# A small early write of zeros to the output, and the last store moved to the SP queue, in a one-core lp-pool kernel

## The chip, the cores and the metric

The kernel runs on one core of a Trainium2 chip. The metric is the time of the kernel on the device in microseconds (us), the median of several executions. A profiled execution also leaves a trace, whose span (first to last instruction) is some 2 us shorter than the time; where this text says "span" it means the trace.

## The reference, cut to what matters

An lp pooling with p = 2 over windows of 4: square, mean over 4 neighbours, square root. The input is 32 x 256 x 4096 float32 (134.22 MB), the output a quarter of it (33.55 MB).

```python
for i in range(out_length):
    window = np.abs(x[:, :, 4 * i:4 * i + 4]) ** 2.0
    result[:, :, i] = np.mean(window, axis=-1) ** 0.5
```

## The kernel before

The input is taken as 32 loads of 4 MB (128 partitions x 8192 floats, 32 KB a row), all issued by the sync engine SP into four slots. Each load is squared in place by ScalarE (ACT), in two halves, summed in fours by VectorE (DVE) into an output tile, and rooted by ACT. Four loads fill one output tile of 4 MB. The first six such tiles are stored from ACT's DMA queue; the last two big ones (called held) are stored from SP's queue, after all loads have been issued; the last output block comes from a single load, is 1 MB, and is stored from ACT.

```python
in_pool = ctx.enter_context(tc.tile_pool(name="in_pool", bufs=4))
out_pool = ctx.enter_context(tc.tile_pool(name="out_pool", bufs=2))
last_pool = ctx.enter_context(tc.tile_pool(name="last_pool", bufs=1))
# [cut]
def root(i, c):
    # [cut]
    nc.scalar.activation(
        out=o, in_=o, func=mybir.ActivationFunctionType.Sqrt, scale=1.0 / k,
    )
    if i == first + g - 1 and c + CH == W and group_of[i] not in held:
        nc.scalar.dma_start(out=out_block(group_of[i]), in_=ot)

for i in range(3):
    load(i)

pending = None
for i in range(n):
    if i + 3 < n:
        load(i + 3)
    # [cut] square, sum, and the root of the half before
root(*pending)
for gi in sorted(held):
    nc.sync.dma_start(out=out_block(gi), in_=ots[gi])
```

## Time and profile before

| before | value |
|---|---|
| time, median | 395.79 us (3 runs, 395.79 to 395.8) |
| span of the trace | 393.7 us |
| bytes moved by DMA | 167.79 MB, mean 426 GB/s over the span |
| DVE / ACT busy | 72% / 75% |

First lines of the page. The digits are the busy tenths of the 16 DMA engines in 40 equal slices (9.84 us each), and GB/s is what they moved in each slice.

```profile
span 393.7 us, 357 instructions
...
DVE 282.8 (72%) x64; ACT 294.7 (75%) x130; POOL 0.2 (0%) x4
...
DMA  8999998999999999999999999999999999999997
GB/s 350 446 430 426 426 426 373 449 446 430 433 426 426 426 430 453 440 430 433 426 426 426 426 449 443 427 433 430 426 426 426 443 446 433 430 433 426 426 435 314
DMA packets 5906, 167.79 MB, mean 426 GB/s; under 512 B 656, under 2 KB 656, under 8 KB 656
```

The reader is to see that the DMA engines are busy from end to end, and that one slice stands out: the seventh, 59 to 69 us, at 373 GB/s where its neighbours have 426 or more.

The longest waits of the two compute engines (engine, line and tile, what was waited for: total us, times, longest).

```profile
DVE ot L112 <- ACT xt L108: 102.6, 38, 16.5
ACT xt L108 <- DMA xt<-in_x_dram: 85.0, 32, 10.9
```

ACT waits for loads, DVE for ACT: the compute engines follow the DMA.

Some lines of the chain of work that ended last, in order of time (start us, us, what).

```profile
2.11 39.87 DMA xt<-in_x_dram
...
54.55 37.06 DMA xt<-in_x_dram
...
104.18 35.91 DMA xt<-in_x_dram
...
152.67 35.95 DMA xt<-in_x_dram
...
249.70 36.50 DMA xt<-in_x_dram
...
347.26 26.27 DMA xt<-in_x_dram
```

A "DMA" entry here is the stretch until a load landed. Nearly the same pattern repeats every 48.5 us, with a load stretch of 35.9 us. Two are longer: the second, which spans the first store (37.06 us), and the sixth (36.50 us). The first, with the start in it, and the last, for one load alone, can't be compared.

The DMA issues of the page (out<-in, queue, count, size of each, median us from issue to landing).

```profile
xt<-in_x_dram SPq DMA_DIRECT2D x32, 4096.0 KB, 35.9
out_dram<-ot ACTq DMA_DIRECT2D x6, 4096.0 KB, 23.2
out_dram<-ot SPq DMA_DIRECT2D x1, 4096.0 KB, 34.1
out_dram<-ot SPq DMA_DIRECT2D x1, 3072.0 KB, 12.3
out_dram<-ot ACTq DMA_DIRECT2D x1, 1024.0 KB, 5.6
```

Below the page lie the records of the single DMA packets. An undisturbed 32 KB load packet takes 1.213 us on one engine. This text calls the *loss* of a stretch the sum of what packets there took above the undisturbed time of their size (1.213 us for 32 KB, 0.912 for 24 KB, 0.309 for 8 KB; only packets over 2% above it count), divided by the 16 engines. Around the first store of this kernel, between 30 and 66 us, that is 1.14 us, of which 1.12 lie between 58 and 62 us. From 66 to 345 us, with five more big stores from ACT's queue, it is 0.06 us.

### The profile page before, as it was taken

The numbers are of one execution on the slowest core, as the hardware profiler recorded it, in microseconds if no ns is written. First come the engines' busy times: TensorE is split into PE (matmuls) and PEld (weight loads), VectorE is DVE, ScalarE is ACT, GpSimd is POOL, SyncE is SP. The second block draws the span as 40 slices with busy tenths as digits, with TensorE's granted clock in tenths as the row PEclk, the third lists the DMA queues.
The fourth block names the chain that finished last, engine by engine and source line by source line (L and its number), as shares of the span: only waits on it lengthen the run. The fifth ranks groups of instructions, "written<-read, shape, count | busy, mean of one in ns | idle before, by whom it ended". The sixth has DMA issues, their size and how long they took to land.

```text
span 393.7 us, 357 instructions
## 1 busy us (share of the span) xinstructions
DVE 282.8 (72%) x64; ACT 294.7 (75%) x130; POOL 0.2 (0%) x4
## 2 busy tenths in 40 slices
DVE  0399996739976399764988559866598846999992
ACT  1699987469883798828988189863998819999981
POOL 0000000000000000000000000000000000000000
DMA  8999998999999999999999999999999999999997
GB/s 350 446 430 426 426 426 373 449 446 430 433 426 426 426 430 453 440 430 433 426 426 426 426 449 443 427 433 430 426 426 426 443 446 433 430 433 426 426 435 314
DMA packets 5906, 167.79 MB, mean 426 GB/s; under 512 B 656, under 2 KB 656, under 8 KB 656
## 3 DMA queue, kind: packets, MB, share of 16 engines
q1 hardware_dynamic: 4896, 141.56, 83.9%
q10 hardware_dynamic: 1008, 26.21, 15.5%
q14 instruction: 2, 0.02, 0.0%
HBM read 134.22 MB, written 33.55 MB: 426 GB/s over the span
## 4 chain that ended last, share of the span: by engine, by line
DMA 72%; ACT 17%; DVE 9%; SPq 0%; issue 0%; ACTq 0%
DMA xt<-in_x_dram 72%; ACT xt L108 14%; DVE ot L112 9%; ACT ot L87 2%; SPq L79 0%; ACTq L108 0%
## 5 line engine op out<-in xcount | busy, mean ns | idle before, releaser
L112 DVE TENSOR_REDUCE ot<-xt 128x1024 f32<-128x4096 f32 x64 | 282.8, 4420 | 103.4 <-ACT xt L108 102.6
L108 ACT ACTIVATE xt<-xt 128x4096 f32<-128x4096 f32 x64 | 230.9, 3610 | 87.6 <-DMA xt<-in_x_dram 85.0
L87 ACT ACTIVATE ot<-ot 128x1024 f32<-128x1024 f32 x64 | 67.0, 1047 | 4.2 <-DVE ot L112 3.4
L108 ACT ACT_TABLE_LOAD x1 | 1.3, 1283 | 0.7 <-PEq L139 0.7
L87 ACT ACT_TABLE_LOAD x1 | 1.3, 1283 | 0.0
L139 POOL MEMSET const-uint8-127<- 128x1 uint8 x1 | 0.1, 102 | 0.0
L139 POOL MEMSET const-bfloat16-1.0<- 128x1 bf16 x1 | 0.1, 101 | 0.0
L139 POOL MEMSET const-float32-0.0<- 128x1 f32 x1 | 0.1, 98 | 0.2 <-issue 0.2
L139 POOL MEMSET const-float32-1.0<- 128x1 f32 x1 | 0.1, 98 | 0.0
## 6 DMA issues: line engine op xcount, KB each, us to landing
xt<-in_x_dram SPq DMA_DIRECT2D x32, 4096.0 KB, 35.9
out_dram<-ot ACTq DMA_DIRECT2D x6, 4096.0 KB, 23.2
out_dram<-ot SPq DMA_DIRECT2D x1, 4096.0 KB, 34.1
out_dram<-ot SPq DMA_DIRECT2D x1, 3072.0 KB, 12.3
out_dram<-ot ACTq DMA_DIRECT2D x1, 1024.0 KB, 5.6
```

Of the source, the lines that this page charges most:

```text
L87: nc.scalar.activation(out=o, in_=o, func=mybir.ActivationFunctionType.Sqrt, scale=1.0 / k,)
L108: nc.scalar.activation(out=xh, in_=xh, func=mybir.ActivationFunctionType.Square,)
L112: nc.vector.tensor_reduce(out=ots[gi][:, at:at + CH // k], in_=xh.rearrange("p (n j) -> p n j", j=k), axis=mybir.AxisListType.X, op=mybir. ...
L139: nc = _bacc.Bacc("TRN2", target_bir_lowering=False, num_devices=1)
```

## The change

The intent: the first write of the program seems to cost something; let a tiny one pay it where the DMA is only starting. It is 8 KB of zeros, 16 rows of 512 B, made by a memset on the GpSimd engine (POOL) and sent from ACT's queue to the last output block, which the last store overwrites later. And the last store goes out on the queue where the other late stores are. The diff rewrites much of the code without changing what it does (same loads, same groups, same order of work). Its core:

```diff
-    LAST = 1
... [cut]
-    held = {len(groups) - 1 - LAST - j for j in range(2)}
+    X_SLOTS, O_SLOTS = 4, 2
+    groups = [4] * 7 + [3, 1]
+    late = {6, 7, 8}
+    in_x = {8}
... [cut]
-        if i == first + g - 1 and c + CH == W and group_of[i] not in held:
-            nc.scalar.dma_start(out=out_block(group_of[i]), in_=ot)
+        if ends and g not in late:
+            store(g, nc.scalar)
... [cut]
+    zero = w_pool.tile([16, 128], fp32, name="zero")
+    nc.gpsimd.memset(zero, 0.0)
+    nc.scalar.dma_start(out=block(of, len(groups) - 1, k)[0:16, 0:128], in_=zero)
... [cut]
-            pool = last_pool if i >= n - LAST else out_pool
-            ot = pool.tile([P, g * W // k], fp32)
+            pool, width = (o_pool, O_W) if g not in in_x else (x_pool, W)
+            t = pool.tile([P, width], fp32, name="ot" if g not in in_x else "xt")
... [cut]
-    for gi in sorted(held):
-        nc.sync.dma_start(out=out_block(gi), in_=ots[gi])
+    for g in sorted(late):
+        store(g, nc.sync)
```

So there are three parts: the zeros; the last store on SP; and, for the sake of space, the last output tile in a used load slot instead of a buffer of its own.

More of the change, by code (lines that the diff above doesn't have):

```diff
@@ L33 @@
     fp32 = mybir.dt.float32
+    Act = mybir.ActivationFunctionType
     xf = x.rearrange("b c l -> (b c l)")
@@ L36 @@
     total = xf.shape[0] // P
-    W = 8192
-    CH = 4096
-    GROUP = 4
-    LAST = 1
-    n = total // W
-    assert n * W == total
-    groups = []
-    i = 0
-    while i < n - LAST:
-        g = min(GROUP, n - LAST - i)
-        groups.append((i, g))
-        i += g
-    groups += [(j, 1) for j in range(n - LAST, n)]
-    held = {len(groups) - 1 - LAST - j for j in range(2)}
-    group_of = {}
-    for gi, (first, g) in enumerate(groups):
-        for j in range(g):
-            group_of[first + j] = gi
@@ L59 @@
-    in_pool = ctx.enter_context(tc.tile_pool(name="in_pool", bufs=4))
-    out_pool = ctx.enter_context(tc.tile_pool(name="out_pool", bufs=2))
-    last_pool = ctx.enter_context(tc.tile_pool(name="last_pool", bufs=1))
-    ctx.enter_context(tc.manual_schedule())
-    def x_block(i):
-        first, g = groups[group_of[i]]
-        block = xf[first * W * P:(first + g) * W * P].rearrange("(p w) -> p w", p=P)
-        return block[:, (i - first) * W:(i - first + 1) * W]
-    def out_block(gi):
-        first, g = groups[gi]
-        return of[first * W * P // k:(first + g) * W * P // k].rearrange("(p w) -> p w", p=P)
@@ L74 @@
-    xts = {}
-    ots = {}
-    def load(i):
-        xt = in_pool.tile([P, W], fp32)
-        nc.sync.dma_start(out=xt, in_=x_block(i))
-        xts[i] = xt
-    def root(i, c):
-        first, g = groups[group_of[i]]
-        ot = ots[group_of[i]]
-        at = ((i - first) * W + c) // k
-        o = ot[:, at:at + CH // k]
-        nc.scalar.activation(
-            out=o, in_=o, func=mybir.ActivationFunctionType.Sqrt, scale=1.0 / k,
-        )
-        if i == first + g - 1 and c + CH == W and group_of[i] not in held:
-            nc.scalar.dma_start(out=out_block(group_of[i]), in_=ot)
@@ L93 @@
-    for i in range(3):
-        load(i)
+    W, O_W = 8192, 8192
+    X_SLOTS, O_SLOTS = 4, 2
+    slots = [[(W, [4096, 4096])]] * 32
+    groups = [4] * 7 + [3, 1]
+    late = {6, 7, 8}
+    in_x = {8}
+    loads = [(s, sum(w for w, _ in slot[:j]), *slot[j]) for s, slot in enumerate(slots)
+             for j in range(len(slot))]
+    n = len(loads)
+    assert sum(w for _, _, w, _ in loads) == total
+    firsts = [sum(groups[:g]) for g in range(len(groups))]
+    assert sum(groups) == n
+    group_of = [g for g, count in enumerate(groups) for _ in range(count)]
@@ new lines, with block @@
+    columns = [sum(w for _, _, w, _ in loads[firsts[g]:firsts[g] + groups[g]])
+               for g in range(len(groups))]
+    x_pool = ctx.enter_context(tc.tile_pool(name="x_pool", bufs=X_SLOTS))
+    o_pool = ctx.enter_context(tc.tile_pool(name="o_pool", bufs=O_SLOTS))
+    w_pool = ctx.enter_context(tc.tile_pool(name="w_pool", bufs=1))
+    ctx.enter_context(tc.manual_schedule())
+    def block(flat, g, div):
+        at, width = sum(columns[:g]) * P // div, columns[g] * P // div
+        return flat[at:at + width].rearrange("(p w) -> p w", p=P)
@@ new lines, with load, store, root @@
+    slot_tiles = {}
+    xs = {}
+    def load(i):
+        s, at, w, _ = loads[i]
+        if at == 0:
+            slot_tiles[s] = x_pool.tile([P, W], fp32, name="xt")
+        v = slot_tiles[s][:, at:at + w]
+        g = group_of[i]
+        src = sum(loads[j][2] for j in range(firsts[g], i))
+        nc.sync.dma_start(out=v, in_=block(xf, g, 1)[:, src:src + w])
+        xs[i] = v
+    ots = {}
+    def store(g, queue):
+        queue.dma_start(out=block(of, g, k), in_=ots[g])
+    def root(g, o, ends):
+        nc.scalar.activation(out=o, in_=o, func=Act.Sqrt, scale=1.0 / k)
+        if ends and g not in late:
+            store(g, nc.scalar)
@@ L96 @@
+    zero = w_pool.tile([16, 128], fp32, name="zero")
+    nc.gpsimd.memset(zero, 0.0)
+    nc.scalar.dma_start(out=block(of, len(groups) - 1, k)[0:16, 0:128], in_=zero)
+    ahead = 0
+    while ahead < n and loads[ahead][0] < X_SLOTS - 1:
+        load(ahead)
+        ahead += 1
     pending = None
     for i in range(n):
-        if i + 3 < n:
-            load(i + 3)
-        gi = group_of[i]
-        first, g = groups[gi]
-        if i == first:
-            pool = last_pool if i >= n - LAST else out_pool
-            ot = pool.tile([P, g * W // k], fp32)
-            ots[gi] = ot
@@ L106 @@
-        for c in range(0, W, CH):
-            xh = xts[i][:, c:c + CH]
-            nc.scalar.activation(
-                out=xh, in_=xh, func=mybir.ActivationFunctionType.Square,
-            )
-            at = ((i - first) * W + c) // k
+        s, _, w, chunks = loads[i]
+        while ahead < n and loads[ahead][0] < s + X_SLOTS:
+            load(ahead)
+            ahead += 1
+        g = group_of[i]
+        if i == firsts[g]:
+            pool, width = (o_pool, O_W) if g not in in_x else (x_pool, W)
+            t = pool.tile([P, width], fp32, name="ot" if g not in in_x else "xt")
+            ots[g] = t[:, 0:columns[g] // k]
@@ L112 @@
+        at = sum(loads[j][2] for j in range(firsts[g], i)) // k
+        assert sum(chunks) == w
+        c = 0
+        for step in chunks:
+            v = xs[i][:, c:c + step]
+            nc.scalar.activation(out=v, in_=v, func=Act.Square)
+            o = ots[g][:, at + c // k:at + (c + step) // k]
             nc.vector.tensor_reduce(
-                out=ots[gi][:, at:at + CH // k],
-                in_=xh.rearrange("p (n j) -> p n j", j=k),
+                out=o, in_=v.rearrange("p (n j) -> p n j", j=k),
@@ L118 @@
                 root(*pending)
-            pending = (i, c)
+            c += step
+            pending = (g, o, i == firsts[g] + groups[g] - 1 and c == w)
     root(*pending)
-    for gi in sorted(held):
-        nc.sync.dma_start(out=out_block(gi), in_=ots[gi])
+    for g in sorted(late):
+        store(g, nc.sync)
 _INS = ['x', 'p', 'kernel_size']
```

## The prediction

> What bounds the kernel now. The page of before shows a span of 393.7 us, ACT busy 75%, DVE 72%, and the DMA row at 9 tenths in nearly every slice: 167.79 MB at a mean of 426 GB/s. The chain that ended last is 72% loads, and ACT's biggest wait is for loads (85.0 us, 32 times). In the packet records one 32 KB packet takes 1.213 us on an engine, with 16 engines 433 GB/s. The Trainium skill, "DMA: Bandwidth & Descriptors", section "Where 436 GB/s comes from", puts the port ceiling at 435 GB/s; this trace agrees (433). At that rate the bytes alone need about 387 us, so some 6 us can be won without fewer bytes; faster by over 2% (7.9 us) is all but excluded.
>
> Where those 6 us are. About 1.75 us before the first data packet; 0.6 us extra in each engine's first packet; 1.2 us after the last; small gaps; and two disturbances. (a) When the first store starts (issued on ACT at 56.4 us), one load packet on every engine takes 2.1 to 2.36 us, and the next ones a little more: about 1.1 us lost on all 16 engines. It is the slice at 373 GB/s, and the load chain there is 37.06 us against 35.9 in later groups. No later store does this. So the first write of the program pays 1.1 us, once. (b) When the last store (1 MB, 8 KB packets, ACT queue) starts at 388.9 us, some packets take 0.4 to 0.75 in place of 0.309 us, 0.2 us on the mean.
>
> What the change does. Loads, groups, arithmetic and the big stores stay; the last output tile moves into a free load slot, which waits for nothing. Added: a POOL memset (about 0.1 us, by the others on the page), one ACT DMA issue (0.34 to 0.37 us) while ACT has 10.9 us of idle before the first load lands, and 8 KB of traffic (0.02 us at 433 GB/s). None of it is on the critical path by itself. The intent is to pay (a) at 2 to 3 us, beside the first load. A stall that hits running load packets there costs as much as before; only the part that overlaps the start of the first load (idle until 1.75 us, then 0.6 us extra) is saved. ACT waits for POOL, so I put its issue at 1.0 us and the write at 2.0 to 2.3 us: I expect half to all of it hidden, gain 0.3 to 1.1 us.
>
> The last store on SP waits for the same root, is issued within 0.1 us of the old 387.26 us, and queues behind the 3 MB store that drains until 388.9 us. The skill, same page, section "Issuing engines are not separate DMA queues", says both queues run on the same 16 engines; I expect 0 to 0.2 us gain, from (b).
>
> Predicted: 395.0 us, a gain of 0.8 us (0.2%); 8 in 10 between 394.3 and 395.9. Faster by over 2%: 0.01; within 2%: 0.98; slower by over 2%: 0.01.
>
> What would show it. The slice near 59 to 69 us back at about 426 GB/s, no packet over 1.3 us where the first big store begins; the first load landing equal or later (12.1 us now); landings after the first store about 1 us earlier; the last store landing in 5.6 us or slightly less.
>
> What would make it wrong. The stall merely moves to the first load (gain near 0); it belongs to the first large store or the first block written, not to the first write, so it stays; or the zeros' write delays the first load by more than it saves (up to 1 us slower).

## The result

| | before | after |
|---|---|---|
| time, median of 6 runs | 395.73 us (395.5 to 395.8) | 395.53 us (395.4 to 395.79) |
| ratio | | 0.9996, 95% interval 0.9984 to 1.0009 |
| span of the trace | 393.7 us | 393.5 us |
| loss at the first big store (packet records) | 1.14 us | 0.95 us |

A ratio is the mean time of one kernel's fast runs over that of the other's of the same rounds, so not quite the ratio of the medians. The interval holds 1: no gain is shown, and one of more than 0.2% is all but excluded.

The profile after, same views. First the page.

```profile
span 393.5 us, 360 instructions
...
DVE 282.8 (72%) x64; ACT 294.7 (75%) x130; POOL 0.4 (0%) x5
...
DMA  8999999999999999999999999999999999999997
GB/s 347 453 426 426 426 426 403 443 430 430 426 426 426 433 450 443 427 433 426 426 426 430 440 446 436 427 430 426 426 430 430 446 440 433 430 430 426 426 436 314
DMA packets 5938, 167.80 MB, mean 426 GB/s; under 512 B 672, under 2 KB 688, under 8 KB 688
```

The seventh slice is at 403 GB/s in place of 373, still below its neighbours at 426 and 443.

The longest waits, with a new line for ACT's start. Its 1.4 us are not all a wait for the memset of the zeros, which was over at 0.93 us: they are ACT's idle time before its table load, in which the issue of the zeros (0.38 us) is not counted as busy, and in before the same idle time was 0.7 us. It ends long before the first load is there.

```profile
DVE ot L115 <- ACT xt L113: 101.4, 37, 16.4
ACT xt L113 <- DMA xt<-in_x_dram: 84.1, 32, 10.1
...
ACT L113 <- POOL zero L91: 1.4, 1, 1.4
```

The chain of work that ended last.

```profile
2.12 39.75 DMA xt<-in_x_dram
...
54.44 36.91 DMA xt<-in_x_dram
...
103.91 35.93 DMA xt<-in_x_dram
...
152.41 35.97 DMA xt<-in_x_dram
...
346.93 26.29 DMA xt<-in_x_dram
```

The load stretch across the first big store is 36.91 us, against 37.06 before and 35.9 to 36.0 in the undisturbed ones (the sixth, with an instruction fetch in it, is 36.41). The stall that was to be paid early is still there.

The DMA issues.

```profile
out_dram<-xt SPq DMA_DIRECT2D x1, 1024.0 KB, 5.6
out_dram<-zero ACTq DMA_DIRECT2D x1, 8.0 KB, 5.7
```

And the start in order of time (start us, us, engine and line, what).

```profile
0.74 0.19 POOL L91 MEMSET zero<- 16x128 f32 x1 [0.29 <-POOLq L142]
0.74 2.01 SPq L77 DMA_DIRECT2D xt<-in_x_dram  x4
0.96 0.38 ACTq L92 DMA_DIRECT2D out_dram<-zero  x1
...
12.73 7.12 ACT L113 ACTIVATE xt<-xt 128x4096 f32<-128x4096 f32 x2 [10.08 <-DMA xt<-in_x_dram]
```

The zeros were issued at 0.96 us and landed 5.7 us later. Their sixteen packets took up to 0.027 us each and ran between 4.68 and 5.12 us. No load packet of the first 30 us, past each engine's first, took over 1.22 us, so nothing was paid there: the loss of the stretch 3 to 30 us is 0.00.

The difference of the two spans adds up so: the last load is issued 0.33 us earlier (346.93 against 347.26; by the chain, 0.11 of it was there before the stretch with the first big store, 54.44 against 54.55, 0.16 comes from that stretch and the compute after it, and 0.06 from the stretches that follow); from there to the last data packet it is 45.23 against 45.21 us; and from the last data packet to the end 1.34 against 1.20 us. Sum: 0.33 - 0.02 - 0.14 = 0.17 us, by the unrounded spans 0.18.

### The profile page after: what moved, and what is told of

It reads as the page before. It is cut to its first block, busy times and chain, and to the rows that moved or that the text cites. A ratio compares the mean times of both kernels' runs of the same rounds, so it can differ in the third digit from the quotient of the medians.

```text
span 393.5 us, 360 instructions
## 1 busy us (share of the span) xinstructions
DVE 282.8 (72%) x64; ACT 294.7 (75%) x130; POOL 0.4 (0%) x5
## 4 chain that ended last, share of the span: by engine, by line
DMA 72%; ACT 17%; DVE 9%; SPq 0%; issue 0%; ACTq 0%
DMA xt<-in_x_dram 72%; ACT xt L113 15%; DVE ot L115 8%; ACT ot L86 2%; DVE xt L115 1%; SPq L77 0%; ACT xt L86 0%; ACTq L113 0%
## 5 line engine op out<-in xcount | busy, mean ns | idle before, releaser
L115 DVE TENSOR_REDUCE ot<-xt 128x1024 f32<-128x4096 f32 x62 | 273.9, 4419 | 102.2 <-ACT xt L113 101.4
L86 ACT ACTIVATE ot<-ot 128x1024 f32<-128x1024 f32 x62 | 64.9, 1046 | 0.8
L115 DVE TENSOR_REDUCE xt<-xt 128x1024 f32<-128x4096 f32 x2 | 8.8, 4419 | 0.9 <-ACT xt L113 0.9
L86 ACT ACTIVATE xt<-xt 128x1024 f32<-128x1024 f32 x2 | 2.1, 1056 | 3.4 <-DVE xt L115 3.4
## 6 DMA issues: line engine op xcount, KB each, us to landing
xt<-in_x_dram SPq DMA_DIRECT2D x32, 4096.0 KB, 35.9
```

What stands on the lines that cost most here:

```text
L86: nc.scalar.activation(out=o, in_=o, func=Act.Sqrt, scale=1.0 / k)
L115: nc.vector.tensor_reduce(out=o, in_=v.rearrange("p (n j) -> p n j", j=k), axis=mybir.AxisListType.X, op=mybir.AluOpType.add,)
```

## The experiments

Twelve runs followed, one of them (e8) the kernel of before once more. The numbers of all traces, worked out from the packet records and the instructions in the same way, stand in one table. "Early" is the loss from 3 to 30 us, "first big store" that from 30 to 66 us, "slow last" the packets of the 1 MB last store (of 128) over 0.35 us; "to data" is the time from the issue of the last load to the end of the last data packet, "after data" from there to the end of the span.

```
kernel                      zeros        last  early  first big  slow   to     after
                                         on           store      last   data   data
before                      none         ACT   0.02   1.14       14     45.21  1.20
before, second trace        none         ACT   0.00   1.19       15     45.22  1.20
after                       16 x 512 B   SP    0.00   0.95       0      45.23  1.34
e1_zero_only                16 x 512 B   ACT   0.00   1.11       0      45.21  1.34
e2_sp_only                  none         SP    0.00   0.97       0      45.23  1.20
e3_zero_first_block         16 x 512 B   SP    0.00   0.93       0      45.22  1.35
e4_first_store_early        16 x 512 B   SP    0.00   0.88       0      51.87  1.36
e5_zero_1mb                 128 x 8 KB   SP    0.39   0.12       0      45.22  1.35
e6_zero_128_rows            128 x 512 B  SP    0.00   1.12       0      45.22  1.34
e7_first_store_sp           none         SP    0.01   0.00       0      45.97  1.16
e9_zero_16_long_rows        16 x 8 KB    SP    0.00   0.98       0      45.22  1.34
e10_zero_256kb              128 x 2 KB   SP    0.01   1.05       0      45.22  1.35
e11_slot_only               none         ACT   0.00   0.90       13     45.22  1.20
e12_before_last_sp          none         SP    0.02   1.06       0      45.21  1.20
```

The row of e7 has 0.00 for the first big store because there the loss falls outside the window, at 77 to 80 us (0.66 us, see e7). Each kernel but before has one trace here.

My theory after the result was that the zeros do nothing, because the loss belongs to the first *large* store and not to the first write. Its rival was that the zeros went to the wrong place or queue: a first touch of the block, the partitions or the packet length that the big store uses.

### e1_zero_only: the zeros without the SP queue

```diff
-    late = {6, 7, 8}
+    late = {6, 7}
```

> The changed kernel, but the last store goes back to ACT's queue; the zeros stay. If the zeros brought the small gain (about 0.2 us in time): 395.5 us as with the whole change, the load chain across the first big store 36.9 us as there, and the last store's packets undisturbed (none over 0.32 us), since its block has been touched. If the store queue brought it: the time of before, some packets of the last store again at 0.4 to 0.75 us.

Measured: 395.8 us (5 runs, 395.77 to 396.13) against 395.8 of before, ratio 1.0003 (0.9991 to 1.0016). Load stretch across the first store 37.04 us. The slow packets of the last store are gone, yet the stretch to the last data packet is 45.21 us as in before. So the zeros bring nothing, and the slow packets had cost nothing: one engine is behind the others at the end (in before it finished at 392.48 us, all others by 391.93). The slow packets of before started between 389.5 and 390.0 us; the late engine came to the last store only at 390.03 us, and its packets took 0.309 us.

What makes that engine late stands in the traces. A packet record does not name its engine, but each packet starts within some ns of the end of the one before it, so an engine can be followed. In before an 8 KB fetch of instructions takes 0.333 us at 250.83 us, and the load packet behind it takes 1.875 in place of 1.213 us. Followed from there, this engine lands its part of the sixth stretch's load at 285.73 us, the other fifteen theirs by 285.13, and it is the engine that ends the kernel last (in e11 and e12 every step to the end is free of doubt; in e4 and e7 the end is another). The fetch at 159.76 us is on another engine, done by 391.89 us. So the sixth stretch, 36.4 to 36.7 us in all traces but e7's (35.98, where the fetch's cost does not show), loses about half as much as the first store costs, before and after, and the change doesn't touch it.

### e2_sp_only: the SP queue without the zeros

```diff
-    zero = w_pool.tile([16, 128], fp32, name="zero")
-    nc.gpsimd.memset(zero, 0.0)
-    nc.scalar.dma_start(out=block(of, len(groups) - 1, k)[0:16, 0:128], in_=zero)
```

> The changed kernel without the zeros; the last store stays on SP. If the store queue brought the small gain: 395.5 us, no packet of the last store over 0.32 us, and the stall at the first store back at 1.1 us (load chain 37.06 us). If the zeros brought it: the time of before, and the last store's packets at 0.4 to 0.75 us again.

Measured: 395.57 us (5 runs, 395.43 to 395.7) against 395.8, ratio 0.9995 (0.9981 to 1.0009). The first-store loss did not come back to 1.1; it is 0.97 us without any zeros, the same as with them. So the 0.95 of the changed kernel was not the zeros' doing. I took the 0.2 us of this kernel as a hint that the SP queue helps, but the trace does not show where: the stretch to the last data packet, where the queue is used, is 45.23 us.

### e3_zero_first_block: the zeros to the block that is stored first

```diff
-    nc.scalar.dma_start(out=block(of, len(groups) - 1, k)[0:16, 0:128], in_=zero)
+    nc.scalar.dma_start(out=block(of, 0, k)[0:16, 0:128], in_=zero)
```

> The changed kernel with the zeros sent to the first block in place of the last. Theory A, the stall belongs to the first touch of the output block that is stored: it is gone at the first store (load chain 35.9 us, no packet over 1.3 us there) and the kernel gains another 0.9 us, 394.6. Theory B, it belongs to the first large store whatever was touched: unchanged, about 0.95 us lost there, 395.5 us.

Measured: 395.61 us (4 runs, 395.4 to 396.08), ratio 0.9998 (0.9985 to 1.0012), loss 0.93 us. Theory B: which block the small write touches does not matter.

### e4_first_store_early: the first big store sooner

```diff
-    groups = [4] * 7 + [3, 1]
-    late = {6, 7, 8}
-    in_x = {8}
+    groups = [2] + [4] * 7 + [1, 1]
+    late = {7, 8, 9}
+    in_x = {9}
```

> The changed kernel with groups of 2, 4 x 7, 1, 1 loads, so that the first big store (2 MB) is issued at about 37 us in place of 56. If the stall follows the first big store: slow packets (over 1.5 us) at 38 to 41 us and none at 57 to 60. If it comes at a time of its own: at 57 to 60 us as before.

Measured, one look, state unknown: the slow packets (over 1.5 us) start at 38.6 us, and none is at 57 to 60. The line of GB/s by slice (9.92 us each):

```profile
GB/s 361 433 423 423 395 451 423 423 436 449 436 423 423 427 449 436 433 423 423 446 439 433 426 423 433 444 433 433 423 423 446 439 433 426 423 433 443 436 407 188
```

The low slice is now the fifth (395, 40 to 50 us), and the seventh is an undisturbed 423. The loss goes with the first big store. The time is 398.81 us, for a reason that has nothing to do with this: with last groups of one load each, less is left to store when the loads end, and the last slices run at 407 and 188 GB/s.

### e5_zero_1mb: a large write of zeros

```diff
-    zero = w_pool.tile([16, 128], fp32, name="zero")
+    zero = w_pool.tile([P, W // k], fp32, name="zero")
     nc.gpsimd.memset(zero, 0.0)
-    nc.scalar.dma_start(out=block(of, len(groups) - 1, k)[0:16, 0:128], in_=zero)
+    nc.scalar.dma_start(out=block(of, len(groups) - 1, k), in_=zero)
```

> The changed kernel with the whole last block (1 MB, 128 partitions of 8 KB) written with zeros at the start, which costs 2.4 us of DMA time by itself (1 MB at 433 GB/s). If the loss of about 1 us belongs to the first store of some size, it shows at the start as packets of over 1.5 us within some us of this write, and is gone at 57 to 61 us (load chain there 35.9). If it belongs to the first store that meets a full load queue, or to the kernel's first real block, about 1 us is still lost at 57 to 61 us.

Measured, one look, state unknown: 397.53 us. The chain, and the issue of the zeros:

```profile
2.11 42.75 DMA xt<-in_x_dram
...
57.43 35.91 DMA xt<-in_x_dram
...
105.91 35.90 DMA xt<-in_x_dram
```

```profile
out_dram<-zero ACTq DMA_DIRECT2D x1, 1024.0 KB, 16.8
```

The stretch across the first big store (from 57.43 us) is 35.91 us, as undisturbed ones are: the loss there is 0.12 us. It moved to the early write, where load packets took up to 1.458 us in three places between 6 and 14 us, 0.39 us in all. My expectation of packets over 1.5 us at the start was wrong: the loss there comes in three parts and is smaller. So a write can take the loss away from the first store, if it is large enough; but this one costs 2.4 us of DMA time to save some 0.5 us (1.0 less 0.39 and 0.12), and the kernel is 1.7 us slower than before.

### e6_zero_128_rows: all partitions, short rows

```diff
-    zero = w_pool.tile([16, 128], fp32, name="zero")
+    zero = w_pool.tile([P, 128], fp32, name="zero")
... [cut: the store covers all 128 partitions]
```

> The changed kernel with zeros of 128 partitions x 512 B (64 KB, eight packets on each engine) in place of 16 x 512 B. If the first store's loss comes from the first use of all partitions or of eight descriptors for each engine: gone at 57 to 61 us, and up to 0.9 us faster than the changed kernel (394.6) where the start hides it. If it comes from the amount written: about 1 us lost at 57 to 61 us as before, 395.5 us.

Measured: 395.79 us (4 runs, 395.66 to 395.94), ratio 1.0002 (0.9987 to 1.0017), loss at the first big store 1.12 us. Using all partitions and eight packets an engine is not enough.

### e7_first_store_sp: the first big store on the other queue

This is e2 with one more edit:

```diff
-            store(g, nc.scalar)
+            store(g, nc.sync if g == 0 else nc.scalar)
```

> Without zeros, last store on SP, and the first big store on SP's queue too, behind the loads. If the loss belongs to the first use of ACT's queue: nothing at the first store and about 1 us at the second (issued at about 105 us on ACT). If it belongs to the first write in the program whatever its queue: slow packets soon after the first store's issue at 56 to 58 us or where its packets start, and none at the second. Time 395.5 to 395.8 us either way.

Measured: 396.14 us with a wide spread (395.27, 395.53, 396.76, 397.4; ratio 1.0004, 0.9982 to 1.0025), so its time says nothing. The trace, which was the slowest of the four, has its line of GB/s so (slices of 9.89 us):

```profile
GB/s 365 431 424 424 424 437 447 391 424 454 434 424 428 424 428 447 438 428 434 424 424 431 437 447 431 422 424 431 431 451 414 441 431 424 428 441 431 424 428 248
```

The low slice is the eighth (391, 69 to 79 us). The store was issued at 56.3 us behind queued loads, and the loss, 0.66 us, is at 77 to 80 us, when by the load rate its turn in the queue came; nothing is lost at 56 to 62 us. The next store, the first on ACT's queue, lost 0.08 us. So the loss belongs neither to the issue of a store nor to the first use of ACT's queue. The small losses later in this trace (together about 0.9 us) were in no other trace and are not explained.

### e8_before_again: the kernel of before, second trace

No edit.

> The kernel of before once more, for its spread: how much the loss at the first store (1.12 us in the first trace), the slow packets of the last store (0.22 us) and the load chain across the first store (37.06 us) vary from one execution to the next. If they are the kernel's own, they come back within 0.05 us; if they are chance, they differ by about as much as the changed kernel's did (0.95 against 1.12).

Measured, one look, state unknown: 395.95 us; loss at the first store 1.19 us (1.14 in the first trace), slow packets of the last store 15 (14), load stretch 37.12 us (37.06). Both come back. So, as far as one repeat can show, the loss is no chance of one execution. Between 0.90 and 1.19 us it varies from trace to trace (whether by kernel or by execution is not shown), but not with the zeros: with small or mid-size zeros 0.95, 1.11, 0.93, 1.12, 0.98, 1.05 (mean 1.02), without 1.14, 1.19, 0.97, 0.90, 1.06 (mean 1.05).

### e9_zero_16_long_rows and e10_zero_256kb: between 8 KB and 1 MB

```diff
-    zero = w_pool.tile([16, 128], fp32, name="zero")
+    zero = w_pool.tile([16, 2048], fp32, name="zero")   # e9, 128 KB
+    zero = w_pool.tile([128, 512], fp32, name="zero")   # e10, 256 KB
... [cut: the store is cut to match]
```

> The changed kernel with zeros of 16 partitions x 8 KB (128 KB, one 8 KB packet on each engine, 0.3 us of DMA time). If long packets are what makes a first write pay (the 1 MB of zeros did with 8 KB packets, the 64 KB with 512 B packets didn't): the loss at the first big store falls to 0.2 us, with at most 0.4 us lost at the start, and 395.3 us or less. If it is the amount written: about 1 us at the first big store as before, 395.8 us or a little more.

Measured: 395.87 us (4 runs), ratio 1.0004 (0.9989 to 1.0019), loss 0.98 us. One long packet on each engine is not it.

> The changed kernel with zeros of 128 partitions x 2 KB (256 KB, eight 2 KB packets on each engine, 0.6 us of DMA time). If the loss depends on the amount written so far: part of the 1 us is gone at the first big store (between the 1.1 us of 64 KB and the 0.2 us of 1 MB) and the time is 395.8 us or a little more, since the zeros cost 0.6 us. If it is the length of a packet: as with 64 KB, 1.1 us at the first big store and 396.2 us.

Measured: 396.2 us (4 runs), ratio 1.0013 (0.9997 to 1.003), loss 1.05 us. Both runs, and all before, fit a loss that only a write of more than 256 KB, or one with many 8 KB packets on each engine, takes over. Which of the two is not settled; the 1 MB also took longer from issue to landing (16.8 us, e10 14.6 us), and no run holds size and duration apart.

### e11_slot_only and e12_before_last_sp: the two other parts alone

e11 is the changed kernel with both `late = {6, 7}` and the three lines of the zeros taken out. e12 is the kernel of before with this edit:

```diff
-        if i == first + g - 1 and c + CH == W and group_of[i] not in held:
+        if i == first + g - 1 and c + CH == W and group_of[i] not in held and group_of[i] != len(groups) - 1:
... [cut]
-    for gi in sorted(held):
+    for gi in sorted(held) + [len(groups) - 1]:
```

> The changed kernel without the zeros and with the last store back on ACT's queue: of the change only the last output tile's place in a load slot is left. If the slow packets of the last store (14 and 15 of 128 over 0.35 us in the two traces of before, none in any kernel with the tile in a load slot) come from the tile's place: none here. If the zeros or the SP queue removed them: 14 or 15 again. On the clock, if the 0.2 us of the kernels with the last store on SP comes from that queue: 395.8 us; if from the tile's place: 395.6 us.

Measured: 395.52 us (5 runs, 395.18 to 395.75) against 395.66, ratio 0.9996 (0.9982 to 1.0009). 13 slow packets in the last store, so the tile's place does not remove them; the zeros (e1) or the SP queue (e2, e12) do, each alone, in one trace each; how is not shown.

> The kernel of before with nothing changed but the last store, on SP's queue behind the two held ones. If that queue brings 0.2 us: 395.6 us, against 395.8 for before, and no sign of it in the stretch from the last load's issue to the end (46.4 us in before and in the kernel with SP but no zeros). If the last tile's place or chance brings it: 395.8 us.

Measured: 395.62 us (5 runs, 395.28 to 395.63) against 395.66, ratio 0.9996 (0.9983 to 1.0008), 45.21 us to the last data. With the last store on ACT (e11) or on SP (e12, e2) the ratio is the same 0.9995 or 0.9996, and every interval holds 1. My hint of e2, that the SP queue is worth 0.2 us, falls.

## Why the prediction was right or wrong

The time was right: 395.0 us was said with a range of 394.3 to 395.9, 395.53 was measured, and "within 2%" came in. For the expected gain that is luck of a wide range: before itself, at 395.73 us, lies in it, so a change that does nothing would have been right too. The reason for the range, that the DMA is busy from end to end at 426 of at most 433 GB/s, holds after the change too (426 GB/s, chain 72% loads). But most of the small gain was forecast from a step that failed.

- **The step that failed: "So the first write of the program pays 1.1 us, once."** It is the first large store that pays, wherever it falls (from 38.6 us in e4, from 77 us in e7). A write of 8 KB paid nothing, wherever it went (after, e1, e3), and neither did 64, 128 or 256 KB (e6, e9, e10); each of these left 0.93 to 1.12 us at the first big store. Only 1 MB of zeros took it over (e5). The prediction named this as a way to be wrong ("it belongs to the first large store or the first block written, not to the first write, so it stays"), and the first half of that is what the runs show. The gain of 0.3 to 1.1 us from it was 0. The moment was missed as well: the issue came at 0.96 us (1.0 was said), but the zeros' packets ran at 4.68 to 5.12 us and not at 2.0 to 2.3, after the start that was to hide them.
- **"None of it is on the critical path by itself"**: nearly right. At the start it holds; the first load was squared at 12.73 to 12.83 us with the 8 KB of zeros (after, e1, e3) and at 12.77 to 12.91 without (before twice, e2, e11, e12). But the end of the span is 0.14 us longer in each of the eight traces with zeros (1.34 to 1.36 us after the last data, against 1.16 to 1.20 in the six without). The trace shows how: at the end SP waits for the semaphore of each DMA in turn. In before the wait for the last store is the last one. With one DMA more the order of the waits is another, and two more wait instructions follow the one that the last store released, some 0.06 us each.
- **The last store on SP, "0 to 0.2 us gain, from (b)"**: the low end was right, and the reason for the rest was wrong. The slow packets (b) do vanish, but from the issue of the last load to the last data it takes 45.21 to 45.23 us with and without them, in twelve of the fourteen traces (all but e4, whose last groups differ, and the uneven e7). The Trainium skill, "DMA: Bandwidth & Descriptors", section "Issuing engines are not separate DMA queues", says that DMAs of either queue end up on the same 16 engines; these 45.21 to 45.23 us agree.
- **What remains of the 0.2 us.** It is not shown to be a gain. In the trace it is 0.11 us up to the first big store, 0.16 us across it and 0.06 us after it, less 0.14 us of wait at the end and 0.02 us before it. The start of the stretch with the first big store varies as much among the kernels without zeros (54.44 us in e12 to 54.59 in e2), and so does the loss there. What makes the first-store loss 0.90 in one kernel and 1.19 in another, and what the loss is inside the DMA, stays open.

No version beat both kernels beyond the noise.

## What to carry to other kernels

When a trace shows a cost at a "first" event, say which property of the event you think it hangs on (the first write, the first large one, the queue, the place, the moment) and vary one at a time before you build a workaround: here the small writes, taken together, had the queue, the block, the partitions and the 8 KB rows, and only a large one took the cost over. The slow packets of the last store cost nothing here, since the engine that ended last was not among the slowed ones, so measure from a fixed event to the last byte. And one more DMA, however small, may also be one more semaphore that the end of the kernel waits for.

## What the Trainium skill lacked or had wrong

- "DMA: Bandwidth & Descriptors" has nothing on the cost of the first large store: 0.90 to 1.19 us lost on all 16 engines, by load packets that took up to 2.43 in place of 1.213 us (e8), 0.88 where that store had 2 MB; writes of up to 256 KB did not take it over, one of 1 MB did.
- The same page, section "Queues, rings and completion order", says that an engine drains a whole packet of about 9 to 17 descriptors from one ring before it switches (a packet record of the trace is one row). The measurement differs: beside a queue full of 32 KB rows the eight 512 B rows of each engine (e6) went out one at a time, about one for each 32 KB load packet of 1.213 us, spread over 4.7 to 12.6 us: 64 KB took 13.2 us from issue to landing, the 8 KB 5.7 us.
- No page read says what one more DMA adds to the waits at the end of a kernel: it made the end 0.14 us longer, about 0.06 us for each wait instruction that came after the one that the last store released.
- Nothing wrong was found in one figure that the prediction used, the port ceiling of 435 GB/s in section "Where 436 GB/s comes from" of the same page: 32 KB in 1.213 us on each of 16 engines is 432 GB/s. No more of that section is meant.
